# Stores, first output weights and second norm in another order around the last mLSTM head, and query columns converted one projection earlier

## The chip, the cores and the metric

The kernel runs on one core of a Trainium2 chip. A core has a matrix engine (TensorE, PE in the profile, with its weight loads as PEld), a vector engine (VectorE, DVE), a scalar engine (ScalarE, ACT), a general engine (GpSimd, POOL) and a sync engine (SyncE, SP), which here issues most of the transfers. ACT and POOL can issue transfers too. Every engine works through its own instructions in order; they wait for each other at semaphores. The metric is device time of one execution in microseconds (us); the kernel before takes 1564.69 us (median of three runs).

## The reference

One layer of a diffusion backbone works on 128 context tokens and 1024 latent tokens of width 1024. Attention heads and mLSTM heads (a bidirectional matrix-memory scan in chunks of 128 tokens) stand side by side; their outputs are merged by one projection, `w_out`, and a gated feed-forward layer follows.

```python
def trunk_layer(x, mods, ...):
    h = rmsnorm(x, norm1_w) * (1 + sc1) + sh1
    aq, ak, av, mq, mk, mv, mo, mg = jnp.split(h @ w_in, SPLIT_POINTS, axis=-1)
    ...
    attn_o = attention(aq, keys, vals)
    ...
    hm, st_f, st_b = mlstm_bidir(heads(mq), heads(mk) * (MLSTM_DK ** -0.5), heads(mv), gates, init_f, init_b)
    hm = rmsnorm(hm.transpose(0, 2, 1, 3), mlstm_norm_w.reshape(MLSTM_HEADS, MLSTM_DV))
    hm = (hm.reshape(B, T, MLSTM_WIDTH) * jax.nn.sigmoid(mo.astype(F32))).astype(x.dtype)
    mix = jnp.concatenate([attn_o, hm], axis=-1) @ w_out
    x = x + g1 * mix
    h2 = rmsnorm(x, norm2_w) * (1 + sc2) + sh2
    x = x + g2 * swiglu(h2, w_gu, w_down)
    return x, ak, av, st_f, st_b
```

There are 8 query heads and 2 key/value heads of width 64, and 4 mLSTM heads of width 128. Besides the two outputs the kernel returns the new keys, values and mLSTM states.

## The kernel before

**Tiles.** The 1152 tokens are 9 blocks of 128 rows (`NB`), in 3 chunks of 3 (`NCH`, `CB`; `CT` = 384 columns). Numbers are split into a high and a low part, and each product is taken as three: high by high, high by low, low by high. For `w_in` the parts are 16-bit (`Scaled`, which also finds a power-of-two scale from the largest absolute value); for `w_out`, `w_gu` and `w_down` they are 32-bit (`load_piece`: load into `raw`, cast on ACT to the high part at L152, subtract on DVE at L137 to the low part).

**Order.** The program is written as generators that yield between small steps; `weave` and `beside` run a main one and side ones at given rates, and `emit` runs one to its end. A planner then orders each engine's instructions by a simulated timeline (`schedule_with_timeline_sim`) and the order of the program; `hot(n)` raises the priority of what it encloses. A buffer with a `tag` and `bufs` is used again when its last reader is done, and memory of a closed pool is used again by pools opened later: the first tiles of the output stage lie where tiles of the mLSTM stage were.

**mLSTM heads.** `head_project(h)` computes head `h`'s queries, keys, values and output gate from four weight pieces of 1024 columns: each has two rows of 512 columns, 128 of them for each of the four. `pairs` converts a piece: ACT writes the high part (L218) and DVE the low one in one instruction (L219); for every second piece ACT scales in place (L221) and casts (L222), and DVE subtracts (L137). `q_group` takes the query columns for the three chunks (L809 to L811); then `linear_tok` (L483 to L485) takes the other 384 columns for each of the nine blocks, with `evac`, the transpose of the keys, the copy `kT` (L768) and `update`, which carries the forward state on (L793). Meanwhile `ready` loads the next head's pieces and finds their scale. `pairs` of a head is written at the start of its `head_project`; head 0's stands ahead of all of them (`groups_in[1].made`). The scan of a head, `head_mlstm`, is woven into the projection of the next one. It works block by block (`weights` with `dt` at L850 and `sd` at L852; products at L867 and L874; the result `hm` at L887 and L888, its scaling by POOL at L891 and L897) and stores `hm` to `hm_d` at L899: for the last head in three parts, part 0 from SP and parts 1 and 2 from ACT, for the others all at the end from SP. `hm_d[c]` has a row per token and 512 columns, 128 for each head.

**The last head.** Beside the scan of head 3 run `ada_rest((5,))`, which makes the last modulation rows, and `out` of `attn_out_first`: the first half of the output projection (rows of `w_out` for the attention part) for chunk 0, in two column halves `n`. It loads two weight pieces per half, and after half 1 of block `i` the finished rows `x1[:, i]` are put on a list, `stores`; when all is written out, ACT stores them to `x1a_d` (L1464).

**Prefill.** `prefill` takes the second half of the output projection (the mLSTM part) for all nine blocks: `load_hm` reads a block of `hm_d`, two blocks ahead; `mix` transposes and splits it (L116, L1185); `half(b, n)` makes 12 products (L1145 to L1147) with weights `ws[n]` and adds them to the rows; `end(b)` takes the sum of squares of a block of chunk 0 (L1303) and, for `b` from 1 to 3, runs `norm2` (L1319 and on) of block `b - 1`, which transposes the normed rows for the feed-forward layer. The attention of chunk 1 is woven in between. `ws[0]` is loaded first; `ws[1]` follows the loads of the first rows, all on SP. After the prefill come the feed-forward products (L1340 to L1342, then L1117 to L1119), chunk by chunk.

Of the kernel before, what the change touches and what calls it, by code (L numbers as in the profile page):

```python
# [8 lines left out]
F32 = mybir.dt.float32  # L9
# [10 lines left out]
P = 128  # L20
# [25 lines left out]
def hybrid_step(ctx: ExitStack, tc: tile.TileContext, I: dict, O: dict):  # L46
# [57 lines left out]
        return psum["mm"].tile([P, 512], F32, name=nm("mm"), tag="mm")  # L104

    q_d = [drp.tile([P, 512], F32, name=f"q_d{b}") for b in range(NB)]
    hm_d = [drp.tile([CT, 512], F32, name=f"hm_d{c}") for c in range(NCH)]
    g_d = drp.tile([2, 2, D], F32, name="g_d")
    x1a_d = [drp.tile([P, D], F32, name=f"x1a_d{i}") for i in range(CB)]
    x1_d = [drp.tile([P, D], F32, name=f"x1_d{i}") for i in range(CB)]  # L110
# [68 lines left out]
    class Scaled:  # L179


        def __init__(self, srcs, shape, raws=None):
            self.srcs, self.shape, self.raws, self.made = srcs, shape, raws, None

        def ready(self):

# [24 lines left out]
        def pairs(self, dve_every=2):  # L211
# [12 lines left out]
                out.append(tuple(v.rearrange("p (a b) -> p a b", b=b) for v in (hi, lo)))  # L224
            return out


    scale1 = cp.tile([P, KD, 2], F32, name="scale1")
    shift1 = cp.tile([P, KD, 2], F32, name="shift1")
# [514 lines left out]
    def head_project(h, st):  # L744

        w = groups_in[h + 1]
        pieces = w.made or w.pairs()
        w.inverses()
        nxt_steps = groups_in[h + 2].ready() if h + 1 < NH else iter(())
        next(nxt_steps, None)  # L750
        st["q"] = [None] * NCH
        st["b"] = [None] * NB
# [1 line left out]
        def evac(b, ps):  # L754
            kt = mlp.tile([P, P], F32, name=nm("kt"), tag="kt", bufs=2)
            act(kt, ps[:, 0:P], AF.Copy, scale=w.inv_k)
            va = mlp.tile([P, P + 1], F32, name=nm("va"), tag="va", bufs=MB)
            act(va[:, 0:P], ps[:, P : 2 * P], AF.Copy, scale=w.inv)
            pool.memset(va[:, P : P + 1], 1.0)
            th = mlp.tile([P, P], F32, name=nm("th"), tag="th", bufs=1)  # L760
            act(th, ps[:, 2 * P : 3 * P], AF.Tanh, scale=w.inv_half)
            so = mlp.tile([P, P], F32, name=nm("so"), tag="so", bufs=MB)
            pool.tensor_tensor(out=so, in0=th, in1=mwh[:, h * P : (h + 1) * P], op=ALU.mult)
            pool.tensor_tensor(out=so, in0=so, in1=mwh[:, h * P : (h + 1) * P], op=ALU.add)
            pt = bank()
            transpose(pt[:, 0:P], kt)
            kT = mlp.tile([P, P], F32, name=nm("kT"), tag="kT", bufs=MB)
            nc.scalar.copy(kT, pt[:, 0:P])  # L768
            st["b"][b] = (kT, va, so)
            update(b, kt, va)  # L770

# [8 lines left out]
        def update(b, kt, va):  # L780
# [6 lines left out]
            for d in range(2):  # L787
                if b == (NBL if d == 0 else 1):
                    continue
                add = pc[:, d * (P + 1) : (d + 1) * (P + 1)]  # L790
                cn = mlp.tile([P, P + 1], F32, name=nm("cs"), tag="cs", bufs=CSB)
                if d == 0 and b > 0:
                    dve.scalar_tensor_tensor(out=cn, in0=states[0, b], scalar=decb[:, b * 4 + h : b * 4 + h + 1], in1=add,  # L793
                                             op0=ALU.mult, op1=ALU.add)
                    states[0, b + 1] = cn
                    continue
                nc.scalar.copy(cn, add)
                if b > 0:
# [27 lines left out]
    def head_mlstm(h, st):  # L826
# [30 lines left out]
        for b in range(NB):  # L857
# [34 lines left out]
            if b in ends:  # L892
                b0 = ends[b]
                n = b + 1 - b0
                v = hm[:, b0 : b + 1, :]
                r = rsqrt(mlp, ssh[:, b0 : b + 1], n, 1.0 / P)
                pool.tensor_tensor(out=v, in0=v, in1=bc(r, 2, [P, n, P]), op=ALU.mult)  # L897
                for c in range(b0 // CB, b // CB + 1):
                    (nc.scalar.dma_start if h == NH - 1 and c > 0 else dma)(hm_d[c][:, h * P : (h + 1) * P].rearrange("(b p) n -> p b n", p=P), hm[:, c * CB : (c + 1) * CB, :])  # L899
            yield  # L900


# [74 lines left out]
    weave(linear_tok(w_q, 0, 512, evac_q(qp, qcc, qss, qw)), beside((gates, 0.7), (ada, 1.15), (kwork, 0.6), (steps, 0.3)), 40, 40)  # L977
    emit(gates)
    emit(steps)
    groups_in[1].made = groups_in[1].pairs()  # L980
    emit(ada)
    emit(kwork)
    es_r.close()
# [166 lines left out]
    def prefill(cur, nxt):  # L1150
# [4 lines left out]
        def load_hm(b):  # L1155
            if b >= NB:
                return None
            hm = xp.tile([P, 512], F32, name=nm("hmr"), tag="hmr", bufs=2)
            dma(hm, hm_d[b // CB][b % CB * P : (b % CB + 1) * P, :])
            return hm  # L1160

        def load_x1(b):
# [41 lines left out]
        def end(b):  # L1204
            if b < CB:
                with hot(200):
                    cur["rs"] += stats(x1s[0][b : b + 1])
            if 0 < b <= CB:
                yield from norm2(0, cur, b - 1)

        for b in range(2):
            mix(b)
# [15 lines left out]
                yield  # L1228
            yield from end(b)

    def attn_out_first(oT, ready, stores):


        x1 = hTp.tile([P, CB, D], F32, name="x1a", tag="hT2")
# [15 lines left out]
        def out():  # L1250
            for n in range(2):
                cs = slice(n * 512, (n + 1) * 512)
                ws = []
                for j in range(2):
                    rows = w_out[2 * j * P : (2 * j + 2) * P, cs].rearrange("(a p) n -> p a n", p=P)
                    ws.append(load_piece([(full_view, rows)], (2, 512), raw=raws[j], own=(his[j], los[j])))
                for cnd in range(2):
                    dma(gt[:, 2 * n + cnd], g_d[0, cnd : cnd + 1, cs].to_broadcast([P, 512]))
                yield
                for i in range(CB):  # L1260
# [193 lines left out]
    stores = []  # L1454
    first, ada = attn_out_first(oT, done, stores)
    emit(att)
    oT = []
    att = attention(1, oT, set())
# [1 line left out]
    emit(first)  # L1460
    emit(ada)
    emit(scan)
    for out, v in stores:
        nc.scalar.dma_start(out, v)  # L1464
    es1.close()
    es_wp.close()
    es_d.close()
# [121 lines left out]
```

## Time and profile before

| | |
|---|---|
| runs shown, us | 1562.04, 1564.69, 1565.68 |
| profiled execution, us | 1563.28 |
| its span, us | 1561.5 |
| mean granted TensorE clock | 0.98 |
| PE busy | 1484.1 us, 95% of the span |
| DVE busy | 1017.1 us, 65% |
| ACT busy | 772.3 us, 49% |
| POOL busy | 264.9 us, 17% |

The profile is of one execution. Times in the timeline count from the start of the span. A row of the timeline is a start, a duration, engine, line, operation, output and inputs, shapes, a count, and in brackets how long the engine had stood idle and what ended it. "L152" is line 152 of the kernel before. "ACTq" and "SPq" are the queues of ACT and SP when they issue a transfer; such a row's duration is that of the issue, not of the transfer. In a row of stretches a number such as 0.83 behind the five engines is the TensorE clock that was granted, as a share of full speed. A wait for several things is put down to the one that came last.

### The profile page before, as it was taken

Reading aid. Unit: us, or ns where it says so; the run is one execution under the profiler, and the core shown is the slowest. Engines: PE = TensorE matmul, PEld = TensorE weight load, DVE = VectorE, ACT = ScalarE, POOL = GpSimd, SP = SyncE. Lnnn points to the kernel's source line nnn. Section 1 sums busy time; section 2 is a strip of 40 time slices with the busy share of each in tenths; the row PEclk is TensorE's granted clock in tenths of the full one; section 3 lists DMA queues with packets and bytes.
Section 4 is the critical chain, followed back from the end, with each engine's and each line's share of the span. In section 5 each row is a group of like instructions: output and inputs, shape, how many; then the busy total and the mean of one; then the engine's idle time right before and its main releaser. Section 6 shows DMA issues by size and latency. Waiting matters only on the chain.

```text
span 1561.5 us, 23390 instructions
## 1 busy us (share of the span) xinstructions
PE 1484.1 (95%) x8539; PEld 1251.8 (80%) x8539; DVE 1017.1 (65%) x2009; ACT 772.3 (49%) x1413; POOL 264.9 (17%) x352
## 2 busy tenths in 40 slices
PE   6799999999988799999999999999999999999997
PEld 3545567677756679899998989989898989999996
DVE  4977555837648674878655577887866584554554
ACT  4854466847644553555432444556552443323333
POOL 0212423322434242000110101000010101001110
PEclk9999999999999799999999999999999999999999
DMA  9664423523356656797654447878763545544441
GB/s 365 201 179 158 85 70 41 120 49 55 79 183 207 201 111 186 192 192 186 151 151 151 142 132 248 185 169 188 176 159 114 169 131 173 162 121 136 148 141 62
DMA packets 387881, 236.91 MB, mean 152 GB/s; under 512 B 170198, under 2 KB 346790, under 8 KB 387766
## 3 DMA queue, kind: packets, MB, share of 16 engines
q1 hardware_dynamic: 384670, 230.26, 54.6%
q10 hardware_dynamic: 3096, 5.16, 1.3%
q8 instruction: 67, 1.10, 0.3%
q14 instruction: 48, 0.39, 0.1%
HBM read 183.79 MB, written 13.26 MB: 126 GB/s over the span
## 4 chain that ended last, share of the span: by engine, by line
PE 58%; DVE 3%; DMA 1%; ACT 1%; issue 0%; POOL 0%; ACTq 0%; DVEq 0%
PE mm L1341 11%; PE mm L1342 11%; PE mm L1340 11%; PE mm L1117 5%; PE mm L1118 5%; PE mm L1119 5%; PE S L1037 3%; PE po L1062 2%; PE po L1061 1%; PE mm L1145 1%; PE mm L1146 1%; PE mm L1147 1%; DVE wlo L137 1%; DMA raw<-in_w_gu_dram 1%; DVE fl L1329 1%; DVE t L1106 1%
## 5 line engine op out<-in xcount | busy, mean ns | idle before, releaser
L152 ACT CAST whi<-raw 128x1024 fp32r<-128x1024 f32 (+1 forms) x216 | 221.7, 1027 | 386.5 <-PE mm L1341 151.0
L137 DVE TENSOR_TENSOR wlo<-raw,whi 128x1024 fp32r<-128x1024 f32 (+1 forms) x216 | 260.1, 1204 | 178.9 <-ACT whi L152 176.3
L1341 PE MATMUL mm<-aTl,whi 128*128 128x384 f32 x1056 | 355.6, 337 | 2.7 <-DVE aTl L137 2.7
L1342 PE MATMUL mm<-aTh,wlo 128*128 128x384 f32 x1056 | 354.3, 336 | 0.0
L1340 PE MATMUL mm<-aTh,whi 128*128 128x384 f32 x1056 | 353.1, 335 | 0.0
L137 POOL TENSOR_TENSOR hl<-tn,hl 128x384 fp32r<-128x384 f32 x66 | 82.5, 1251 | 847.4 <-ACT hl L1363 776.3
L1341 PEld LDWEIGHTS mm<-aTl,whi 128*128 128x128 f32 x1056 | 198.5, 188 | 4.0 <-DVE aTl L137 3.4
L1340 PEld LDWEIGHTS mm<-aTh,whi 128*128 128x128 f32 x1056 | 198.2, 188 | 0.6
L1342 PEld LDWEIGHTS mm<-aTh,wlo 128*128 128x128 f32 x1056 | 198.4, 188 | 0.1
L1118 PE MATMUL mm<-wlo,hl 128*128 128x512 f32 x372 | 145.6, 391 | 0.0
L1117 PE MATMUL mm<-whi,hl 128*128 128x512 f32 x372 | 144.3, 392 | 0.0
L1119 PE MATMUL mm<-whi,hl 128*128 128x512 f32 x372 | 142.9, 392 | 0.0
L483 PE MATMUL wi<-ipair,hT 128*128 128x384 f16 (+2 forms) x408 | 135.0, 334 | 5.2 <-ACT vall L493 2.8
L484 PE MATMUL wi<-ipair,hT 128*128 128x384 f16 (+2 forms) x408 | 135.0, 334 | 0.0
L485 PE MATMUL wi<-ipair,hT 128*128 128x384 f16 (+2 forms) x408 | 131.6, 334 | 1.0 <-DVE hT L137 1.0
L1044 DVE SCALAR_TENSOR_TENSOR pl<-pr,st,ph 128x1152 f16<-128x1152 f32 (+1 forms) x72 | 96.6, 1342 | 34.5 <-ACT ph L1043 33.0
L1039 DVE TENSOR_REDUCE st<-S 128x1 f32<-128x1152 f32 (+1 forms) x72 | 88.9, 1234 | 15.7 <-PE S L1037 14.8
L1040 ACT ACTIVATE pr<-S,st 128x1152 f32<-128x1152 f32 (+1 forms) x72 | 81.4, 1131 | 31.7 <-DVE st L1039 31.0
L1043 ACT ACTIVATE ph<-pr,st 128x1152 f16<-128x1152 f32 (+1 forms) x72 | 83.8, 1163 | 25.5 <-DVE st L1042 12.7
L1037 PE MATMUL S<-kst,qT 128*128 128x384 f32 (+1 forms) x400 | 87.4, 352 | 1.3 <-ACT pr L1040 0.7
L1106 DVE TENSOR_TENSOR t<-mm,gl 128x512 f32<-128x512 f32 x102 | 68.7, 685 | 27.7 <-DMA gl<-g_d 12.2
L1119 PEld LDWEIGHTS mm<-whi,hl 128*128 128x128 f32 x372 | 69.9, 188 | 14.4
(381 smaller groups left out, 2525.3 us busy)
## 6 DMA issues: line engine op xcount, KB each, us to landing
raw<-in_w_gu_dram SPq DMA_DIRECT2D x132, 512.0 KB
raw<-in_w_down_dram SPq DMA_DIRECT2D x60, 512.0 KB
a<-in_w_ada_dram SPq DMA_DIRECT2D x24, 512.0 KB
gl<-g_d SPq DMA_DIRECT2D x36, 256.0 KB
aw<-in_w_ada_dram SPq DMA_DIRECT2D x16, 512.0 KB
iraw<-in_w_in_dram SPq DMA_DIRECT2D x32, 256.0 KB
raw<-in_w_out_dram SPq DMA_DIRECT2D x12, 512.0 KB
x<-in_x_sample_dram SPq DMA_DIRECT2D x11, 512.0 KB
```

Source lines behind the costliest of these rows:

```text
L137: (dve if eng == "dve" else pool).tensor_tensor(out=out, in0=full, in1=hi, op=ALU.subtract)
L152: nc.scalar.copy(hi[:, :n], raw[:, :n])
L483: mm(ps[:, :n], ah, wh[:, k % 2, c0 : c0 + n], start=(k == 0), stop=False)
L484: mm(ps[:, :n], ah, wl[:, k % 2, c0 : c0 + n], start=False, stop=False)
L485: mm(ps[:, :n], al, wh[:, k % 2, c0 : c0 + n], start=False, stop=(k == KD - 1))
L1037: mm(S[:, n, 0:w], qT[:, h, :], kst[kv][:, t, c0 + n * w : c0 + (n + 1) * w], start=(t == 0), stop=(t == 1))
L1117: mm(ps, ah, wh[:, k % 2, :], start=(k == 0), stop=False)
L1118: mm(ps, ah, wl[:, k % 2, :], start=False, stop=False)
L1119: mm(ps, al, wh[:, k % 2, :], start=False, stop=(k == nk - 1))
L1340: mm(ps, wh[:, k, :], th[:, k, :], start=(k == 0), stop=False)
L1341: mm(ps, wh[:, k, :], tl[:, k, :], start=False, stop=False)
L1342: mm(ps, wl[:, k, :], th[:, k, :], start=False, stop=(k == KD - 1))
```

## The change

Six edits, by place.

- `hm_d[1]` and `hm_d[2]` get the layout (partition, head, 384 columns); `hm_d[0]` stays. A store of one head then writes 384 numbers in a run for each partition, and a load of a block reads four runs of 128.
- The stores of the last head's `hm`: part 0 from SP and part 1 from ACT as before, part 2 from POOL.
- The stores to `x1a_d` are issued by POOL, each right behind the last addition to its rows, instead of by ACT from a list at the end.
- The two weight pieces of each half in `out` are queued, on ACT and on DVE, behind the last `kT` copy and the last forward state update of head 3 (`tc.issue_after`: what is written inside it on that instruction's engine comes behind that instruction).
- In `prefill`, `norm2` of block 0, 1 and 2 follows block 2, 3 and 4 instead of 1, 2 and 3.
- Head weights have four fixed tiles, `head_w`. A new method `part` converts a range of columns of every piece. The query columns (the first 128 of each 512) of head `h + 1` are converted inside `head_project(h)`, behind the search for the scale; the other 384 columns at the start of `head_project(h + 1)`. For head 0 the query columns are converted ahead of the first projection.

```diff
-    hm_d = [drp.tile([CT, 512], F32, name=f"hm_d{c}") for c in range(NCH)]
+    hm_d = [drp.tile([P, NH, CT] if c else [CT, 512], F32, name=f"hm_d{c}") for c in range(NCH)]
...
+        def part(self, tiles, cs):
+            b = self.shape[1]
+            for j, (raw, w) in enumerate(zip(self.raws, tiles)):
+                hi, lo, v = (t.rearrange("p (a b) -> p a b", b=b)[:, :, cs] for t in (w[:, 0], w[:, 1], raw))
+                if j % 2 == 0 or cs.start == 0:
+                    act(hi, v, AF.Copy, scale=self.scale)
+                    dve.scalar_tensor_tensor(out=lo, in0=v, scalar=self.scale, in1=hi, op0=ALU.mult, op1=ALU.subtract)
+                else:
+                    act(v, v, AF.Copy, scale=self.scale)
+                    nc.scalar.copy(hi, v)
+                    sub(lo, v, hi, "dve")
+                yield
...
-        pieces = w.made or w.pairs()
+        pieces = [tuple(v.rearrange("p (a b) -> p a b", b=4 * P) for v in (t[:, 0], t[:, 1])) for t in head_w]
+        emit(w.part(head_w, slice(P, 4 * P)))
         w.inverses()
-        nxt_steps = groups_in[h + 2].ready() if h + 1 < NH else iter(())
+        nxt_steps = chain(groups_in[h + 2].ready(), groups_in[h + 2].part(head_w, slice(0, P))) if h + 1 < NH else iter(())
...
-            nc.scalar.copy(kT, pt[:, 0:P])
+            st["act"] = nc.scalar.copy(kT, pt[:, 0:P])
...
-                    dve.scalar_tensor_tensor(out=cn, in0=states[0, b], scalar=decb[:, b * 4 + h : b * 4 + h + 1], in1=add,
+                    st["dve"] = dve.scalar_tensor_tensor(out=cn, in0=states[0, b], scalar=decb[:, b * 4 + h : b * 4 + h + 1], in1=add,
...
-                    (nc.scalar.dma_start if h == NH - 1 and c > 0 else dma)(hm_d[c][:, h * P : (h + 1) * P].rearrange("(b p) n -> p b n", p=P), hm[:, c * CB : (c + 1) * CB, :])
+                    if c == 0:
+                        dma(hm_d[0][:, h * P : (h + 1) * P].rearrange("(b p) n -> p b n", p=P), hm[:, 0:CB, :])
+                    else:
+                        ((None, nc.scalar.dma_start, pool.dma_start)[c] if alone else dma)(hm_d[c][:, h], hm[:, c * CB : (c + 1) * CB, :].rearrange("p b n -> p (b n)"))
...
-    groups_in[1].made = groups_in[1].pairs()
+    head_w = [wp.tile([P, 2, 1024], F16, name=f"headw{j}", tag="ipair", bufs=4) for j in range(4)]
+    emit(groups_in[1].part(head_w, slice(0, P)))
...
-            dma(hm, hm_d[b // CB][b % CB * P : (b % CB + 1) * P, :])
+            if b < CB:
+                dma(hm, hm_d[0][b * P : (b + 1) * P, :])
+            else:
+                dma(hm.rearrange("p (h n) -> p h n", n=P), hm_d[b // CB][:, :, b % CB * P : (b % CB + 1) * P])
...
-            if 0 < b <= CB:
-                yield from norm2(0, cur, b - 1)
+            if 2 <= b < CB + 2:
+                yield from norm2(0, cur, b - 2)
...
-                    ws.append(load_piece([(full_view, rows)], (2, 512), raw=raws[j], own=(his[j], los[j])))
+                    with tc.issue_after(sts[-1]["act"].ins), tc.issue_after(sts[-1]["dve"].ins):
+                        ws.append(load_piece([(full_view, rows)], (2, 512), raw=raws[j], own=(his[j], los[j])))
...
-                        stores.append((x1a_d[i], x1[:, i]))
+                        pool.dma_start(x1a_d[i], x1[:, i])
...
-    for out, v in stores:
-        nc.scalar.dma_start(out, v)
```

More of the change, by code (lines that the diff above doesn't have):

```diff
@@ L182, in __init__ @@
         def __init__(self, srcs, shape, raws=None):
-            self.srcs, self.shape, self.raws, self.made = srcs, shape, raws, None
+            self.srcs, self.shape, self.raws = srcs, shape, raws
         def ready(self):
@@ L1229, in prefill, with attn_out_first @@
             yield from end(b)
-    def attn_out_first(oT, ready, stores):
+    def attn_out_first(oT, ready):
         x1 = hTp.tile([P, CB, D], F32, name="x1a", tag="hT2")
@@ L1453, in hybrid_step @@
     scan = head_mlstm(NH - 1, sts[NH - 1])
-    stores = []
-    first, ada = attn_out_first(oT, done, stores)
+    first, ada = attn_out_first(oT, done)
     emit(att)
```

## The prediction

> **What bounds the kernel now.** I read the page first, then the busy time in stretches of 10 us between 180 and 700 us, then who waited for whom between 440 and 570 us, and then the timeline at the waits found.
>
> ```profile
> PE 1484.1 (95%) x8539; PEld 1251.8 (80%) x8539; DVE 1017.1 (65%) x2009; ACT 772.3 (49%) x1413; POOL 264.9 (17%) x352
> ...
> PE   6799999999988799999999999999999999999997
> ...
> PEclk9999999999999799999999999999999999999999
> ```
>
> TensorE (PE) sets the time: it is busy for 95% of the span, so no more can be won than its idle time and what a lowered clock costs it. Behind the start-up both lie in the 12th to 14th of the 40 slices (429 to 547 us): the end of the last mLSTM head and the prefill of the output projection. The change touches these and the borders between heads. The stretches, in columns of window, length, busy time of PE, PEld, DVE, ACT and POOL, granted clock, DMA share and GB/s:
>
> ```profile
> 280.00:290.00 10.00, 7.48 (x44) 5.10 (x43) 8.53 (x15) 10.00 (x23) 2.32 (x5) 0.97 0.66 158
> 290.00:300.00 10.00, 10.00 (x48) 7.60 (x49) 7.49 (x21) 9.58 (x30) 5.34 (x11) 0.69 0.41 112
> ...
> 360.00:370.00 10.00, 8.40 (x53) 5.90 (x51) 8.65 (x15) 9.47 (x22) 2.76 (x9) 1.00 0.19 37
> ...
> 450.00:460.00 10.00, 6.80 (x36) 4.65 (x36) 6.27 (x17) 6.70 (x19) 1.84 (x5) 0.83 0.77 271
> ...
> 500.00:510.00 10.00, 2.16 (x13) 1.51 (x11) 7.12 (x24) 4.46 (x10) 3.08 (x4) 0.72 0.85 293
> ...
> 520.00:530.00 10.00, 5.46 (x26) 4.30 (x24) 8.58 (x14) 4.76 (x6) 5.67 (x3) 0.92 0.97 297
> 530.00:540.00 10.00, 5.94 (x21) 5.17 (x22) 5.92 (x31) 7.92 (x14) 1.30 (x2) 0.50 0.27 78
> 540.00:550.00 10.00, 10.00 (x57) 8.28 (x56) 8.67 (x14) 5.65 (x9) 6.33 (x5) 0.90 0.63 85
> 550.00:560.00 10.00, 8.78 (x47) 7.08 (x46) 9.16 (x22) 6.90 (x11) 3.41 (x3) 1.00 0.55 101
> ```
>
> Every hole is followed by a lowered clock (0.69, 0.83, 0.50), so a hole costs more than its own length. The waits of PE, ACT and SyncE's queue (total, times, longest) name the holes:
>
> ```profile
> PE mm L116 <- ACT y L1319: 8.8, 2, 7.9
> PE mm L1145 <- ACT mx L1185: 7.1, 1, 7.1
> PE mm L116 <- ACT it L870: 3.5, 1, 3.5
> PE mm L844 <- DVE sd L852: 2.3, 1, 2.3
> ...
> ACT mx L1185 <- POOL hm L897: 4.0, 1, 4.0
> ACT ir L152 <- DMA ip<-in_w_out_dram: 3.4, 1, 3.4
> ...
> SPq L151 <- DMA hm_d<-hm: 8.0, 1, 8.0
> ```
>
> **The change part by part.** Four holes are dealt with, in order of time.
>
> *Borders between heads.* The conversion of a head's weights costs, over eight pieces (min/median/max ns):
>
> ```profile
> L218 ACT ACTIVATE ipair<-iraw,isc x8: 1132/1156/1180, 149.6 to 366.3; 128x1024 f16<-128x1024 f32 x8
> L219 DVE SCALAR_TENSOR_TENSOR ipair<-iraw,isc,ipair x8: 1274/1284/1549, 150.8 to 369.6; 128x1024 f16<-128x1024 f32 x8
> L222 ACT CAST ipair<-iraw x8: 1029/1062/1099, 151.1 to 368.8; 128x1024 f16<-128x1024 f32 x8
> ...
> 370.68 0.33 PE L809 MATMUL wi<-hT,ipair 128*128 128x384 f16 x1
> 370.84 0.33 PE L810 MATMUL wi<-hT,ipair 128*128 128x384 f16 x1
> ```
>
> Four pieces a head: ACT 4 x 1.156 + 2 x 1.062 = 6.7 us, VectorE (DVE) 4 x 1.284 = 5.1 (its plain subtracts counted as long as L219). All of it stands at the border now, where ACT is full (10.00 of 10 at 280:290). Afterwards a quarter, the query columns, is done inside the preceding projection, and three quarters (ACT 5.1, DVE 3.9) are first needed after the query products, which are 72 products (3 chunks x 8 x 3) 0.16 us apart, 11.5 us of cover. Added is the fixed cost of splitting: eight more instructions a head, at most 0.3 us each by scaling, on engines that are not full away from the border: nothing on the path; if they had no cover, some 2 us a head. The holes at two borders are 2.52 + 1.60 us, and the clock of 0.69 takes another 0.31 x 10 = 3.1. Together 7.2. PE also waits there for copies of the attention and of the last blocks, which stay: I take 5.0, bounds 1 and 7.2.
>
> *First output weights.* The cast of the first `w_out` piece stands on ACT ahead of the end of the last projection and waits for its load:
>
> ```profile
> 450.11 1.04 ACT L152 CAST ir<-ip 128x1024 fp32r<-128x1024 f32 x1 [3.38 <-DMA ip<-in_w_out_dram]
> 452.35 0.33 PE L116 MATMUL mm<-ident,kt 128*128 128x128 f32 x1 [3.46 <-ACT it L870]
> 458.07 0.27 ACT L768 COPY kT<-mm 128x128 f32<-128x128 f32 x1
> ```
>
> Queueing it behind the last `kT` copy (458.07, which itself comes sooner) and its subtract behind the last forward update ends the 3.4 us wait; the clock of 0.83 after it is worth another 0.17 x 10 = 1.7. Late next is the hole at 460 us (2.3, PE waits for `sd`): two casts of 1.04 on ACT and two subtracts of 1.2 on DVE now land just before it, and `dt` and `sd` are queued behind them. That gives back between 0 and 2.5; I take 2.0, as DVE is what PE waits for there. Net 3.1, bounds 0.5 and 5.
>
> *Stores.* ACT stands behind the last store, and SyncE's queue behind the landing of the same store:
>
> ```profile
> 494.73 0.33 ACTq L1464 DMA_DIRECT2D x1a_d<-x1a  x1
> ...
> 496.93 0.62 ACT L850 ACTIVATE dt<-mm,QT 128x128 f32<-128x128 f32 x2 [5.55 <-PE wi L867]
> ...
> 502.35 1.98 ACT L152 CAST whi<-raw 128x1024 fp32r<-128x1024 f32 x2
> ...
> 507.88 0.38 ACTq L899 DMA_DIRECT2D hm_d<-hm  x1
> 508.30 1.07 ACT L1185 CAST mx<-mm 128x512 fp32r<-128x512 f32 x2 [3.97 <-POOL hm L897]
> ...
> 512.19 0.90 SPq L151 DMA_DIRECT2D raw<-in_w_out_dram  x2
> 516.30 1.05 ACT L152 CAST whi<-raw 128x1024 fp32r<-128x1024 f32 x1 [3.77 <-DMA raw<-in_w_out_dram]
> ```
>
> With the store of `hm_d` on GpSimd (POOL), `mx` can be cast at 504.3, when the casts of 502.35 are done: 4.0 us sooner, and PE's first products with it. But the second half of the output weights is loaded only at 512.19, when the store has landed 4.3 us after its issue, since its `raw` buffer lies where `hm` was; its cast starts at 516.30. All loads behind it on SyncE (`hmr`, `x`, `w_gu`) wait too. This is late next, so the 4.0 does not count in full: the products with the first half run sooner and PE then stands for the second. What brings the landing forward is the end of the scan: ACT is free of the three `x1a_d` stores, of which the ones near 495 us cost the `dt` at 496.93 about 1 us. What sets it back is the issue on POOL. No transfer is issued by POOL before, so I bound one from the nearest rows: 0.33 us (the issue on ACT) and, far above, the 3.8 us that the cast waited for half a megabyte to land. I take 1.0, nearer the plain issue. Three `x1a_d` stores ahead of it on POOL are 3 us in the 10 us before 500, where POOL computes 3.79 of 10 (490:500) and the scan's `hm` products queue behind them; they find room. The `hm_d` layout makes runs of 1536 bytes in the store instead of 512, and 512 instead of 2048 in six loads, asked for two blocks ahead: taken as nothing, 0 to 1 us a load without that cover. Net 2.0, bounds -4 (POOL's issue at its upper bound) and +5.
>
> ```profile
> 490.00:500.00 10.00, 9.52 (x51) 7.22 (x50) 8.49 (x27) 3.86 (x13) 3.79 (x4) 1.00 0.81 261
> ```
>
> By the Trainium skill (DMA: Bandwidth & Descriptors, Anatomy of one DMA) a store issued by GpSimd takes about 2.0 us plus its bytes over 436 GB/s, so 2.5 us for these 192 KB against the 4.3 between 507.88 and 512.19. By that figure this part would gain some 2 us more; no run here has shown such a store.
>
> *Second norm one block later.* PE is in order, and the transposes of the first norm stand ahead of block 2:
>
> ```profile
> 519.41 0.39 PE L1147 MATMUL mm<-whi,mx 128*128 128x512 f32 x1
> 519.64 0.39 PE L1145 MATMUL mm<-whi,mx 128*128 128x512 f32 x1
> ...
> 533.41 1.97 PE L116 MATMUL mm<-ident,y 128*128 128x128 f32 x8 [7.95 <-ACT y L1319]
> ```
>
> Block 2's 24 products at 0.23 us, 5.5 us, and its transposes (0.6) go into this hole of 7.95, if its inputs are there. The hole gone, the clock of 0.50 at 530:540 (5.94 x 0.5 = 3.0) and of 0.90 after it (1.0) mostly goes as well. So 6 to 10 come into reach. Late next is DVE, with 5.92, 8.67 and 9.16 of 10 busy from 530 to 560: only some 6 us of it are free for PE to run ahead into. I take 6.0, bounds 3 and 10. The third norm comes with block 4 of 8, so the first gate and up products, after block 8, do not wait for it: nothing, or one block's 5.5 us if they did.
>
> **Sum.** 5.0 + 3.1 + 2.0 + 6.0 = 16.1 us. The profiled execution took 1563.28 us (span 1561.5 and 1.8 around it); minus 16.1 is 1547.2. The median of the runs, 1564.69, is 1.4 above the profiled one: 1548.6. By the bounds alone: 0.5 to 27.2 us won, some 1537 to 1564 on the median's scale.
>
> **The rivals.**
>
> *Cover runs out sooner.* DVE takes over in the prefill (9.16 of 10 at 550:560 speaks for it) and the second half of the weights eats all of the stores' gain: 3 + 0.5 + 0 + 3.5 = 7 us, 1557.7. Against it: DVE has 4.1 us free just where the hole was.
>
> *Fuller recovery.* No hole means no lowered clock, which is worth as much as half the idle time here: all four near their upper bounds, 7 + 5 + 5 + 10 = 27, 1537.7. Against it: SyncE's 8.0 us wait stays.
>
> *Slower: POOL's issue is dear.* POOL is in order, so the last `hm_d` store stands behind three `x1a_d` stores, and the second half of the weights behind its landing. If one issue holds POOL for T, the three from 490 us on end at 490 + 3T + some 5 us of POOL's own work (3.79 of it in 490:500), then 0.8 for the scaling, T, and 4 to land. With T = 6 that is 524, 12 us after 512.19, and most of the other gains (14) are gone; at about 7 the sign turns; at 8 the landing is near 532, 20 late, and the time 1564.7 + 6 = 1571. For it: POOL's work already stretches when DVE writes beside it, its scaling of 384 columns taking 1.71 us beside a DVE subtract where the one before took 0.83:
>
> ```profile
> 495.64 0.83 POOL L897 TENSOR_TENSOR hm<-hm,ry 128x384 f32<-128x384 f32 x1 [0.94 <-DVE ry L133]
> ...
> 506.14 1.71 POOL L897 TENSOR_TENSOR hm<-hm,ry 128x384 f32<-128x384 f32 x1 [3.16 <-DVE ry L133]
> ```
>
> Against it: that factor of 2 is far from 7 us. The Trainium skill (DMA: Bandwidth & Descriptors, SWDGE vs HWDGE vs iDMA) says that GpSimd writes its descriptors into the on-chip memory itself and that VectorE can lock it out there, which speaks for this rival; the two rows agree in kind, with a factor of 2.
>
> *It does not do what it says.* The order on each engine comes from a planner's simulated timeline; if that puts the moved work back in front of what PE needs, holes move rather than close: 1564. Against it: the norm's place is a data order on PE, and the waits behind the stores are bound to their queue.
>
> **How the numbers follow.** Forecast 0.46, 1548.6, own range 1542 to 1555. Cover runs out 0.24; fuller 0.13; slower 0.10; no change 0.07. No change is within 0.2%, 3.1 us, about what a measurement of this kernel can tell. So faster 0.83, same 0.07, slower 0.10. The range 1536 to 1562 leaves out the slower case, most of no change and a few hundredths of the fuller one.
>
> **What would show it.** Right, if in the changed profile PE waits no more than 1 us at the borders of heads, the cast of the first `w_out` piece follows the last `kT` copy, `mx` is cast within 1 us of the second weight cast, block 2's products precede the first norm's transposes, and the clock in the 14th slice is 9. Wrong, step by step: a wait of PE for `sd` that grows beyond 4 us (weights); POOL busy or silent for several us at a store, with the second weight load later than before relative to the last scan block (stores); DVE above 9 of 10 with PE waiting for it in the prefill (norm). A time above 1562 would make the prediction wrong.

## The result and the profile after

The changed kernel takes 1548.6 us (median of 5 runs, 1546.92 to 1549.49) against 1564.69 before; ratio 0.9902, 95% interval 0.9889 to 0.9914. The profiled execution took 1549.49 us, with a span of 1547.7: 13.8 less than the span before.

The page of the changed kernel first: TensorE has the same instructions and nearly the same busy time (1484.1 us before, 1482.8 now), so what went is above all idle time. Between the start-up and the last slice, the low digits of the clock are now two (8 and 8, in the 13th and 14th slice) where one 7 was.

```profile
PE 1482.8 (96%) x8539; PEld 1248.4 (81%) x8539; DVE 1018.6 (66%) x2025; ACT 772.2 (50%) x1429; POOL 273.9 (18%) x356
...
PE   6899999999998899999999999999999999999997
...
PEclk9899999999998899999999999999999999999998
```

The stretches of the changed kernel, in the columns of the prediction. At the first border between heads (280 to 300) PE still idles, but the clock stays at 1.00. Two big holes are left: one at 490 to 500, ahead of `mx`, and one at 520 to 530, where DVE is busy for 9.67 of 10.

```profile
280.00:290.00 10.00, 8.45 (x56) 6.39 (x55) 9.43 (x20) 9.63 (x25) 6.48 (x11) 1.00 0.33 63
290.00:300.00 10.00, 9.71 (x67) 7.32 (x66) 8.66 (x18) 9.85 (x27) 3.48 (x8) 1.00 0.79 219
...
360.00:370.00 10.00, 9.52 (x59) 6.37 (x57) 8.21 (x17) 9.49 (x22) 4.01 (x6) 1.00 0.31 60
...
450.00:460.00 10.00, 7.62 (x50) 5.16 (x50) 9.97 (x27) 5.00 (x16) 3.85 (x2) 0.83 0.55 175
...
490.00:500.00 10.00, 3.79 (x22) 2.99 (x22) 9.08 (x36) 6.25 (x17) 3.09 (x6) 0.74 0.75 238
500.00:510.00 10.00, 8.96 (x32) 6.77 (x32) 5.58 (x13) 2.83 (x4) 3.40 (x4) 0.75 0.94 327
...
520.00:530.00 10.00, 3.96 (x18) 2.96 (x18) 9.67 (x27) 6.02 (x10) 5.21 (x3) 0.78 0.68 136
530.00:540.00 10.00, 10.00 (x53) 8.48 (x53) 8.84 (x30) 8.33 (x16) 3.27 (x2) 0.71 0.37 80
```

The waits of PE in the changed kernel between 440 and 600 us (total, times, longest). Against before, `mx` fell from 7.1 to 5.2, the longest for `y` from 7.9 to 3.2 and `it` from 3.5 to 0.3. The waits for transposes of the attention grew from 2.5 (`plT`) to 5.0 (`phT`); one of them, of 2.9 us, lies in the same hole as `y`.

```profile
PE mm L1163 <- ACT mx L1206: 5.2, 1, 5.2
PE po L1079 <- DMA phT<-ph: 5.0, 2, 2.9
PE mm L116 <- ACT y L1341: 3.2, 1, 3.2
PE mm L858 <- DVE sd L866: 2.1, 1, 2.1
PE mm L116 <- ACT it L884: 0.3, 1, 0.3
```

**Where the time came from.** A stretch's busy time times its granted clock says how much work PE got done in it; over the whole span that comes to 1463 us in the kernel before and 1462 in the changed one. Summed over the stretches of 10 us:

| stretch | before | after | gained | predicted |
|---|---|---|---|---|
| 270 to 440 us (borders between heads) | 161.7 | 166.7 | 5.0 | 5.0 |
| 440 to 490 us (first output weights) | 40.9 | 45.0 | 4.1 | 3.1 |
| 490 to 660 us (stores, second norm, and what follows) | 140.4 | 145.7 | 5.3 | 2.0 + 6.0 |

That is 14.4 us, of which the start-up takes 1.2 back (232.2 and 231.0 up to 270 us): 13.2 of the 13.8. The start-up differs from one execution to the next (229.9 to 235.7 in the profiles of the kernels below), so these 1.2 us can't be put down to the change. Only the first two of the sum's four terms can be read off this profile, the second roughly: other kernels below that have the weights part get 41.2 to 44.0 us done from 440 to 490. The last two terms stand in one stretch and need experiments; there this execution, the slowest of the five, gained 2.7 us less than the 8.0 of the forecast.

The timeline of the changed kernel around the last head, with the steps that the prediction named. The first `w_out` cast (449.12) follows the last `kT` copy at once (448.83, 9.2 us sooner than the 458.07 of before); `mx` (497.91) follows the second weight cast directly; half of the second weights is asked for at 499.64, before the last `hm_d` store goes out at 502.38.

```profile
448.83 0.27 ACT L782 COPY kT<-mm 128x128 f32<-128x128 f32 x1
449.12 1.05 ACT L152 CAST ir<-ip 128x1024 fp32r<-128x1024 f32 x1
...
482.01 0.71 POOL L1297 DMA_DIRECT2D x1a_d<-x1a  x1
483.87 1.28 POOL L1294 TENSOR_TENSOR x1a<-x1a,gta 128x512 f32<-128x512 f32 x1 [0.66 <-DVE gta L1293]
487.84 0.60 POOL L1297 DMA_DIRECT2D x1a_d<-x1a  x1 [2.69 <-issue]
492.38 0.58 POOL L1297 DMA_DIRECT2D x1a_d<-x1a  x1 [2.63 <-issue]
...
496.96 1.04 ACT L152 CAST whi<-raw 128x1024 fp32r<-128x1024 f32 x1
497.91 1.07 ACT L1206 CAST mx<-mm 128x512 fp32r<-128x512 f32 x2
499.64 1.39 SPq L151 DMA_DIRECT2D raw<-in_w_out_dram  x1
501.15 0.83 POOL L911 TENSOR_TENSOR hm<-hm,ry 128x384 f32<-128x384 f32 x1 [4.20 <-DVE ry L133]
502.38 0.60 POOL L916 DMA_DIRECT2D hm_d<-hm  x1 [0.40 <-POOL hm L911]
```

### The profile page after: what moved, and what is told of

Read it like the earlier page. It is cut to its first block, busy times and chain, and to the rows that moved or that the text cites. A ratio compares the mean times of both kernels' runs of the same rounds, so it can differ in the third digit from the quotient of the medians.

```text
span 1547.7 us, 23430 instructions
## 1 busy us (share of the span) xinstructions
PE 1482.8 (96%) x8539; PEld 1248.4 (81%) x8539; DVE 1018.6 (66%) x2025; ACT 772.2 (50%) x1429; POOL 273.9 (18%) x356
## 4 chain that ended last, share of the span: by engine, by line
PE 83%; DVE 7%; ACT 4%; DMA 4%; issue 2%; POOL 1%; SPq 0%; ACTq 0%; DVEq 0%
PE mm L1363 12%; PE mm L1364 12%; PE mm L1362 12%; PE mm L1135 5%; PE mm L1136 5%; PE mm L1137 5%; PE S L1055 4%; PE wi L498 3%; PE wi L496 3%; PE wi L497 3%; PE mm L1165 2%; PE mm L1163 2%; PE mm L1164 2%; PE po L1079 2%; PE po L1080 2%
## 5 line engine op out<-in xcount | busy, mean ns | idle before, releaser
L496 PE MATMUL wi<-headw,hT 128*128 128x384 f16 x288 | 93.9, 326 | 0.2 <-ACT th L775 0.2
L498 PE MATMUL wi<-headw,hT 128*128 128x384 f16 x288 | 93.9, 326 | 0.0
L497 PE MATMUL wi<-headw,hT 128*128 128x384 f16 x288 | 93.9, 326 | 0.0
L1137 PEld LDWEIGHTS mm<-whi,hl 128*128 128x128 f32 x372 | 69.9, 188 | 14.4
```

Of the source, the lines that this page charges most:

```text
L496: mm(ps[:, :n], ah, wh[:, k % 2, c0 : c0 + n], start=(k == 0), stop=False)
L497: mm(ps[:, :n], ah, wl[:, k % 2, c0 : c0 + n], start=False, stop=False)
L498: mm(ps[:, :n], al, wh[:, k % 2, c0 : c0 + n], start=False, stop=(k == KD - 1))
L1137: mm(ps, al, wh[:, k % 2, :], start=False, stop=(k == nk - 1))
```

## The experiments

Each time is a median of 4 to 11 runs. The kernel before ran beside them three times, with medians of 1563.65 to 1564.38 us. Line numbers are those of each kernel, and a diff may show only the changed expression of a line.

**One part undone.** Four kernels, each the changed one less one part.

Norm:

```diff
-            if 2 <= b < CB + 2:
-                yield from norm2(0, cur, b - 2)
+            if 0 < b <= CB:
+                yield from norm2(0, cur, b - 1)
```

> The changed kernel with one part undone: the second norm stands one block earlier again, behind each block's predecessor. Theory (separate holes, each closed by its own part): PE waits 6 to 8 us again for y at the first norm's transposes, the clock of that stretch falls again, and the time is 6 us over the changed kernel's 1548.6, about 1554.6. Rival (one slack shared by all parts: the prefill is held by DVE or by the second half of the weights, so that PE's hole just lies elsewhere): less than 2 us, 1548.6 to 1550.6.

Weights:

```diff
-                    with tc.issue_after(sts[-1]["act"].ins), tc.issue_after(sts[-1]["dve"].ins):
+                    if True:
```

> The changed kernel with one part undone: the first output weights are cast wherever the planner puts them, no longer behind the last kT copy and the last forward update. Theory (separate holes): ACT waits some 3 us for the load ahead of the last kT copies again, PE waits for it, and the time is 3 us over 1548.6, about 1551.7. Rival (shared slack, the hole returns elsewhere): less than 1 us, 1548.6 to 1549.6.

Stores (there are three `x1a_d` stores, not four as this expectation and a later one say; the list and its loop at the end are those of the kernel before):

```diff
-((None, nc.scalar.dma_start, pool.dma_start)[c] if alone else dma)
+((None, nc.scalar.dma_start, nc.scalar.dma_start)[c] if alone else dma)
...
-                        pool.dma_start(x1a_d[i], x1[:, i])
+                        stores.append((x1a_d[i], x1[:, i]))
```

> The changed kernel with one part undone: the four x1a_d stores and the last hm_d store are issued by ACT again; the new hm_d layout stays. Theory (the forecast's 2 us, and the second half of the weights held back by the landing of the hm_d store): SyncE's queue waits several us for hm_d again, mx is cast some 4 us later against the last scan block, and the time is 2 to 4 us over 1548.6, about 1550.6 to 1552.6. Rival (shared slack: the cover in front of the prefill has grown by the other parts): less than 1 us, 1548.6 to 1549.6, even with the wait back.

Borders:

```diff
-        emit(w.part(head_w, slice(P, 4 * P)))
+        pieces = w.made or w.pairs()
...
-        nxt_steps = chain(groups_in[h + 2].ready(), groups_in[h + 2].part(head_w, slice(0, P))) if h + 1 < NH else iter(())
+        nxt_steps = groups_in[h + 2].ready() if h + 1 < NH else iter(())
...
-    head_w = [wp.tile([P, 2, 1024], F16, name=f"headw{j}", tag="ipair", bufs=4) for j in range(4)]
-    emit(groups_in[1].part(head_w, slice(0, P)))
+    groups_in[1].made = groups_in[1].pairs()
```

> The changed kernel with one part undone: all columns of a head's weights are converted at the border between heads again. Theory (separate holes): PE waits 2.5 and 1.6 us at the two borders again, the clock falls behind the first of them, and the time is 4 to 5 us over 1548.6, about 1553. Rival (shared slack: what the borders win is lost again before the prefill, since the last head's scan sets the pace): less than 2 us, 1548.6 to 1550.6.

Measured:

| undone | median us | ratio to before, interval | over 1548.6 | predicted term |
|---|---|---|---|---|
| norm | 1554.16 | 0.9940, 0.9925 to 0.9956 | 5.6 | 6.0 |
| weights | 1552.40 | 0.9929, 0.9914 to 0.9943 | 3.8 | 3.1 |
| stores | 1551.71 | 0.9925, 0.9911 to 0.9940 | 3.1 | 2.0 |
| borders | 1552.90 | 0.9936, 0.9920 to 0.9952 | 4.3 | 5.0 |

The four differences add to 16.8, and the whole change gave 16.1. Each interval reaches some 2.4 us to either side and that of the changed kernel 2.0, so a difference between two kernels is uncertain by some 3 us and a single row says little. But the rival of one shared slack put every row below 2 us (below 1 for weights and stores), 6 in all, and the four together don't fit it; for the stores row alone the margin is small. The waits come back where they were. Without the norm part, PE's waits show 6.7 us for `y`:

```profile
PE mm L116 <- ACT y L1341: 6.7, 1, 6.7
```

Without the weights part they show the wait for `it` beside the first `w_out` cast:

```profile
PE mm L116 <- ACT it L884: 4.7, 1, 4.7
```

At the borders one detail went otherwise than expected. The stretches of the kernel without the border part show the two holes again (2.67 and 1.57 us), but no lowered clock behind the first:

```profile
280.00:290.00 10.00, 7.33 (x44) 5.11 (x42) 8.71 (x14) 10.00 (x22) 2.45 (x2) 1.00 0.48 126
290.00:300.00 10.00, 9.71 (x65) 7.55 (x66) 7.30 (x23) 9.56 (x31) 5.04 (x14) 1.00 0.63 126
...
360.00:370.00 10.00, 8.43 (x52) 5.90 (x50) 8.80 (x13) 10.00 (x23) 3.24 (x6) 1.00 0.34 66
```

From 270 to 440 us PE got 163.5 us of work done there, 3.2 less than in the changed kernel. That execution is the shortest of its kernel (span 1548.7, runs of 1550.51 to 1557.13). So the clock's part of this term, 3.1 of the 7.2 us in reach, is no fixed price of the hole: it was paid in the profiled execution of before and not in this one. The profiles of all kernels here bear the term out: in the five with the old borders PE gets 161.1 to 163.5 us done from 270 to 440, in the nine with the new ones 165.5 to 166.7.

**The stores taken apart.** The two kinds of store on either engine make four kernels; two were still missing.

Only the last `hm_d` store back on ACT:

```diff
-((None, nc.scalar.dma_start, pool.dma_start)[c] if alone else dma)
+((None, nc.scalar.dma_start, nc.scalar.dma_start)[c] if alone else dma)
```

> The changed kernel with only the last hm_d store back on ACT; the x1a_d stores stay on POOL and the layout is the new one. Theory (the gain of the stores is ACT's program order: the mx cast stands behind a store that waits for POOL's scaling): mx is cast some 4 us after the second weight cast instead of right behind it, PE's wait for mx grows from 5.2 to about 9 us, and nearly the whole 3 us of the stores part returns: 1551 to 1552. Rival (the x1a_d stores beside the scan carry it): 1548.6 to 1549.6.

Only the `x1a_d` stores back on ACT:

```diff
-                        pool.dma_start(x1a_d[i], x1[:, i])
+                        stores.append((x1a_d[i], x1[:, i]))
```

> The changed kernel with only the four x1a_d stores back on ACT; the last hm_d store stays on POOL. Theory (ACT's program order behind the last hm_d store carries the gain): within 1 us of 1548.6, since 0.33 us of issue on an idle ACT delays nothing. Rival (the x1a_d stores beside the scan carry it): the dt of the scan is late again by 1 us a store and the time is 2 to 3 us longer, 1551 to 1552.

Measured, medians in us:

| | last `hm_d` store on POOL | on ACT |
|---|---|---|
| `x1a_d` stores on POOL | 1548.6 (changed kernel) | 1555.05 |
| on ACT | 1547.05 | 1551.71 |

The ratios of the two new kernels are 0.9938 (0.9925 to 0.9951) and 0.9888 (0.9873 to 0.9903). Moving the last `hm_d` store to POOL gains 6.5 or 4.7 us; moving the `x1a_d` stores there gains nothing and may lose 1.6 to 3.3 (in both columns the intervals overlap). The theory of ACT's program order holds, but its sizes were off: the `hm_d` store is worth 6.5 where it said 3, and without the `x1a_d` stores on POOL the time is 1.6 lower where it said within 1. The timeline of the kernel with only the `hm_d` store on ACT shows the order at work: `mx` is ready to be cast behind the weight cast of 499.16, but on ACT the store stands ahead of it, and that waits for POOL's scaling. PE's wait for `mx` grows from 5.2 to 9.6 us. The second half of the weights is late in this kernel too (SyncE's queue waits 4.5 us for the store), but that isn't what costs: between 440 and 660 us PE waits for no output weights in any of the profiles here, apart from 0.4 us in two of them.

```profile
499.16 1.04 ACT L152 CAST whi<-raw 128x1024 fp32r<-128x1024 f32 x1
503.35 0.83 POOL L911 TENSOR_TENSOR hm<-hm,ry 128x384 f32<-128x384 f32 x1 [4.20 <-DVE ry L133]
504.21 0.35 ACTq L916 DMA_DIRECT2D hm_d<-hm  x1
504.60 1.07 ACT L1206 CAST mx<-mm 128x512 fp32r<-128x512 f32 x2 [4.39 <-POOL hm L911]
```

What the `x1a_d` stores cost POOL can be read against the kernel with these stores on ACT, whose timeline has the second store 0.03 us behind the end of the addition that it waits for:

```profile
484.32 1.28 POOL L1294 TENSOR_TENSOR x1a<-x1a,gta 128x512 f32<-128x512 f32 x1 [0.69 <-DVE gta L1293]
485.63 0.33 ACTq L1486 DMA_DIRECT2D x1a_d<-x1a  x1
```

On POOL that addition ends at 485.15 and the issue starts 2.69 us later, marked as a wait for nothing that the profile shows, and takes 0.60; the third store has 2.63 us ahead of it. The issue itself isn't dear, for the first store took 0.71 with nothing ahead. The view of the tile `x1a_d` tells what the others wait for:

```profile
DMA to landing us min/median/max: 4.2/5.5/6.2
```

In order the three stores land after 5.5, 4.2 and 6.2 us: the first at 487.5, the second at 492.1. The second is issued at 487.84 and the third at 492.38, each 0.3 us behind the landing of the store before it. The program as built has no such wait for these stores. It is the same in all the kernels with several stores on POOL: twelve were ready before the last one from POOL had landed, and all twelve started 0.31 us behind that landing. So what costs is not a store on POOL but stores in quick succession. The next additions and the `hm` products queue behind them. Yet the last scaling starts at 501.15 in the changed kernel and at 501.20 without these stores, since it waits for DVE's `ry` in both. SyncE's queue asks for the `x1a_d` rows only at 498.75, behind the landing of the third store, against 494.84 with the stores on ACT; whether the 1.6 us go there, if they are real, stays open.

**The last store alone, on the kernel before.** The store and the load of block 3 and later are written for the new layout as in the change.

```diff
-    hm_d = [drp.tile([CT, 512], F32, name=f"hm_d{c}") for c in range(NCH)]
+    hm_d = [drp.tile([P, NH, CT] if c else [CT, 512], F32, name=f"hm_d{c}") for c in range(NCH)]
...
-(nc.scalar.dma_start if h == NH - 1 and c > 0 else dma)
+((None, nc.scalar.dma_start, pool.dma_start)[c] if alone else dma)
```

> The kernel before with only the new hm_d layout and the last hm_d store on POOL. Theory (ACT's program order): mx is cast right behind the second weight cast near 504.3 instead of at 508.3, the second half of the weights is no longer loaded behind the landing of that store, and the time is 2 to 4 us below the 1564.7 of before. Rival of the record (POOL's issue is dear): the store holds POOL for several us and the time is not below 1564.7. Rival (no use as long as the first norm's hole of 8 us stands behind it): within 1 us of 1564.7.

Measured: 1562.94 us, ratio 0.9990 (0.9979 to 1.0001): 1.4 us, between nothing and 3.3. The mechanism worked in full: the cast of `mx` stands at 504.09, within 0.2 us of the prediction's 504.3, and PE's wait for it fell from 7.1 to 4.0. But PE then stands 7.8 us for `y`, as the waits of this kernel show:

```profile
PE mm L116 <- ACT y L1325: 7.8, 1, 7.8
PE mm L116 <- ACT it L870: 4.4, 1, 4.4
PE mm L1148 <- ACT mx L1191: 4.0, 1, 4.0
```

What starts sooner only waits longer ahead of the first norm's transposes. The same store is worth 6.5 us in the changed kernel, where these stand one block later. That it is the norm's place and not one of the other parts which makes the difference is read from the waits; no kernel has the store and the norm alone.

**The norm alone, on the kernel before.** The edit is the norm's, the other way round.

> The kernel before with only the second norm one block later; stores, weights and borders as they were. Theory (a hole of its own, the prediction's term of 6.0): block 2's products stand ahead of the first norm's transposes, PE's wait of 7.9 us for y falls to 2 to 4, and the time is 5 to 6 us below 1564.7, near 1559. Rival (this part and the stores share one hole, since the last hm_d store alone was worth only 1.4 of the 4.6 to 6.5 us that it is worth in the changed kernel): 1 to 3 us, 1562 to 1564.

Measured: 1553.42 us, ratio 0.9937 (0.9922 to 0.9951): 10.2 us, nearly twice what was expected and two thirds of the whole change. The stretches of this kernel show how: no hole at 520:530, and the clock stays at 1.00 through the hole at 530:540.

```profile
520.00:530.00 10.00, 10.00 (x48) 8.51 (x47) 8.48 (x12) 6.53 (x8) 4.74 (x3) 1.00 1.03 273
530.00:540.00 10.00, 5.11 (x37) 3.88 (x37) 8.66 (x47) 6.30 (x13) 2.48 (x2) 1.00 0.44 109
...
560.00:570.00 10.00, 9.80 (x52) 8.16 (x50) 7.41 (x15) 6.70 (x9) 2.69 (x3) 1.00 0.72 156
```

Against the rows of before (5.46 at 0.92, 5.94 at 0.50, 8.40 at 0.83) that is 5.0, 2.1 and 2.8 us more work done: 9.9 in three stretches. The third wasn't in the prediction. Together with the kernel without the norm part (10.1 us gained by the other three) the parts would give 20.3, and both together give 16.1. They overlap by some 4 us, and the changed kernel shows where: with everything else sooner, DVE is busy for 9.67 of 10 at 520:530, and PE idles there for 6 us again. The `y` that PE waits for at the end of this hole itself waits for `ry`, the last small step of the norm on DVE:

```profile
528.98 1.33 ACT L1341 ACTIVATE y<-x,ry 128x512 f32<-128x512 f32 x2 [0.46 <-DVE ry L133]
```

**The order of two loads, on the kernel before.** In the program as built, transfers of SP and ACT take eight completion semaphores in turn, and a transfer waits until the one eight before it has landed. The first load of the second half of the weights takes the turn of the last `hm_d` store. Its `raw` buffer is one that the first half had, not memory of `hm`. This kernel moves the two loads of that half ahead of two `x1a_d` loads, so that one of them takes the turn.

```diff
         with tc.issue_after(dma(gx_all, g_d[0, 0:1, :].to_broadcast([P, D])).ins):
+            ws.append(out_pieces(1, 1))
             load_x1(0)
             load_x1(1)
-            ws.append(out_pieces(1, 1))
```

> The kernel before with one thing alone: the second half of the output weights is asked for ahead of two of the x1a_d loads. No buffer, store or engine changes. Theory (transfers of SyncE and ACT take eight completion semaphores in turn, and this load waits for the landing of the hm_d store only because its turn falls on the same semaphore): the load goes out near 504 to 507, and the 8.0 us wait for hm_d falls on the x1a_d load that takes the turn instead; the time is 0 to 3 us below 1564.7. Rival, as the prediction on record has it (the raw buffer lies where hm was): the load still waits until the hm_d store has landed, at about 512, and the time stays within 1 us.

Measured: 1566.35 us, ratio 1.0009 (1.0001 to 1.0018). The timeline shows the weights asked for 2.1 us before the store is even issued, into the same buffers as before, and the `x1a_d` loads behind the store:

```profile
508.35 1.83 SPq L151 DMA_DIRECT2D raw<-in_w_out_dram  x2
510.48 0.38 ACTq L899 DMA_DIRECT2D hm_d<-hm  x1
514.61 0.34 SPq L1164 DMA_DIRECT2D x<-x1a_d  x1
```

The waits of SP's queue give the `hm_d` wait to the first of these loads now:

```profile
SPq L1164 <- DMA hm_d<-hm: 4.4, 1, 4.4
```

So the wait follows the turn, not the buffer. That the time doesn't fall may mean that the late weights cost nothing, or that the late `x1a_d` rows cost as much; this time alone doesn't tell. PE's waits in the kernel before speak for the first: none is for the weights. So does the kernel with only the last store on POOL: it has no such wait for either load (the weights go out at 505.60), and `mx` 4 us sooner as well, and all of that was worth 1.4 us.

**One step further.** Three kernels with the `x1a_d` stores on ACT. The first puts both later `hm_d` stores on POOL, the second moves the norm a third block back, the third does both.

```diff
-((None, nc.scalar.dma_start, pool.dma_start)[c] if alone else dma)
+((None, pool.dma_start, pool.dma_start)[c] if alone else dma)
```

> The changed kernel with the x1a_d stores on ACT and, new, both later hm_d stores of the last head on POOL. If ACT's program order behind a store that waits for POOL is what costs, the second weight cast, which there still waits 2.04 us behind the first of these stores, follows the first cast at once, mx is cast some 2 us sooner, and the time is 1 to 2 us below the 1547.05 of the kernel with only the x1a_d stores on ACT, 1545 to 1546. Rival (the last scan blocks hold the engines there, and the hole moves to the next wait): within 1 us, 1546 to 1548.

```diff
-            if 2 <= b < CB + 2:
-                yield from norm2(0, cur, b - 2)
+            if 3 <= b < CB + 3:
+                yield from norm2(0, cur, b - 3)
```

> The changed kernel with the x1a_d stores on ACT and the second norm yet one block later (three blocks behind its block). If the hole before y is only a matter of how far PE runs ahead, the 3.2 us that PE still waits for y vanish, and the time is 2 to 3 us below 1547.05, 1544 to 1545. Rival (DVE is the bound there: 9.67 of 10 busy in the stretch of the hole): the wait moves to the next block's mx or norm, and the time is within 1 us, 1546 to 1548.

> Both edits of the two kernels before this one together. If the holes are separate, their gains add: 1542 to 1545. If DVE bounds the prefill, no better than the better of the two.

Measured: 1546.81 (0.9890, 0.9872 to 0.9908), 1555.59 (0.9949, 0.9932 to 0.9967) and 1554.63 (0.9941, 0.9925 to 0.9957). The rival of the first kernel holds: the wait of PE for ACT's `mx` falls to 2.4, and part of what is saved turns up as a wait for DVE's part of `mx`, as this kernel's waits show. Here too the second store on POOL is issued 0.3 us behind the landing of the first, 2.9 us after its data.

```profile
PE mm L116 <- ACT y L1341: 3.3, 1, 3.3
...
PE mm L1163 <- ACT mx L1206: 2.6, 2, 2.4
PE mm L1165 <- DVE mx L137: 2.4, 1, 2.4
```

The norm yet another block later loses 8 us, which neither theory had. The waits of the kernel with both edits show none for `y`, but four for ACT's `mx` and two for DVE's:

```profile
PE mm L1163 <- ACT mx L1206: 7.0, 4, 3.1
PE mm L1165 <- DVE mx L137: 5.1, 2, 3.0
```

So the hole doesn't close, it moves to the next blocks. Why 8 us are lost stays open: the waits alone don't explain it, since the profiled execution of the second kernel, with 9.2 us for ACT's `mx` and 3.8 for DVE's, took 1547.72, and the other five runs of that kernel 1550.98 to 1557.46. None of these kernels is shown to beat the changed one: 1546.81 and 1547.05 lie below 1548.6, with intervals that overlap its own.

## Why the prediction was right, and where it was not

**The time** came out as forecast, 1548.6. Undone one by one, the sum's parts differ by 0.4 to 1.1 us from the forecast (4.3 for 5.0, 3.8 for 3.1, 3.1 for 2.0, 5.6 for 6.0), which is less than these runs can tell, and each has its own hole, which comes back with it. That the total fits to a tenth is luck: the terms are uncertain by some 3 us each, and one of them came out near its value by another way than the prediction's.

**Borders.** The term was right, its sign only in part: at the first border PE idles for 1.8 us (8.45 and 9.71 of 10), where no single wait is over 1 us. The part that a lowered clock adds differs from one execution to the next. That every hole is followed by a lowered clock was too much already for the prediction's own rows: behind the hole of 1.6 us at 360:370 the clock was 1.00.

**First output weights.** The order came as forecast, the wait for `it` is gone, and "late next", the wait for `sd`, is 2.1 against 2.3 instead of growing. So nothing shows the 2.0 given back; with a term of 3.8 or 4.1 measured against 3.1, they were too many by about 1, if that can be told at all.

**Stores.** This is the step that failed. The prediction wrote that the second half of the weights waits for the landing of the `hm_d` store "since its `raw` buffer lies where `hm` was", that this would be late next, and so halved the gain of 4.0. The swapped loads show that the wait is a turn on a completion semaphore, which in the changed kernel falls elsewhere. Nor does PE stand for the second half: in the kernel before none of its waits is for these weights, and the wait cost little (at most the 1.4 us of the store alone). The gain of the `hm_d` store was then limited by another thing, the first norm's transposes: 1.4 us while these stand first, 4.7 to 6.5 with the norm's move and the other parts. The prediction also took ACT's release from the `x1a_d` stores as a gain; on POOL they are worth nothing or lose up to 3.3 us. So the net of 3.1, near the 2.0 forecast, is a larger gain less a possible loss.

**POOL's issue.** I took 1.0 us. It is 0.4 + 0.6 for the `hm_d` store, as taken. For two of the `x1a_d` stores it is 2.7 + 0.6, since each waits until the store before it has landed, which neither the sum nor the slower rival had; that is still far from the 7 us that this rival needed. The `hm_d` store's time to landing in the changed kernel was longer than the 4.3 that ACT's took, as the last line of the view of this tile shows:

```profile
DMA to landing us min/median/max: 6.9/6.9/6.9
```

It was 6.4 with this store alone and 4.8 with the `x1a_d` stores on ACT. The Trainium skill (DMA: Bandwidth & Descriptors, Anatomy of one DMA) led to an estimate of 2.5 us for such a store; the trace does not agree.

**Norm.** The mechanism and its limit were right: block 2's products fill the hole, and DVE is late next. The prediction's sign of a wrong step, DVE above 9 of 10 with PE waiting for it, is there (9.67 at 520:530), and the part gained all the same. The size depends on the company: 10.2 us alone, at the upper bound; 5.6 beside the other parts, where DVE fills up. I took the limit of 6 for a property of the edit; it is one of the whole change.

**The clock** in the 14th slice is 8, not 9, and 8 in the 13th: the holes before `mx` (5.2 us) and at 520 to 530 are still there.

## What to carry to other kernels

Before a gain from an earlier start is counted, look for the next thing in TensorE's program order that waits for a chain of its own: here one store was worth 1.4 us while such a chain stood in the way and 6.5 in the kernel where it had been moved back. A wait on a transfer need not be about data or buffers; moving a load past one neighbour shows which it is, and TensorE's own waits show whether the late load costs anything at all. A store that waits for another engine is better issued where nothing needed stands behind it in program order. Before several stores in a row are given to POOL, note that here each one was issued only when the one before it had landed, some 4 to 7 us after its own issue.

## What was not expected of the hardware

In the changed kernel the issue of a 512 KB store took POOL 0.58 to 0.71 us; a store that was ready before the last one from POOL had landed started 0.31 us behind that landing, with up to 2.69 us ahead of it in which POOL did nothing that the profile shows. The same store issued by ACT took 0.33 and started 0.03 us behind its data. The granted clock behind a hole of about 2.6 us was 0.69 in one execution and 1.00 in another, of a kernel with the same instructions at that place.
